# Attention tiles laid out by when they are first written, in a fused attention and recurrence block on one Trainium2 core

## The chip, the cores and the metric

The kernel runs on one core of one Trainium2 chip, as a single launch. Times are device microseconds (us) of that core. The kernel before was timed in three runs: 908.11, 908.41 and 908.92 us, median 908.41 us. One further run was profiled; it took 910.35 us, and the profile's span of it is 908.6 us.

## The reference

One layer of a decoder block over 1024 tokens of width 1024, batch 1, all in f32:

```python
h = rmsnorm(x, norm_g) * (1 + scale) + shift            # shift, scale, gate = c @ w_ada + b_ada
q, k, v, g_attn, xr, g_rnn, m_attn, m_rnn = split(h @ w_in)
y_attn = window_attention(rope(q), rope(k), v, sinks) * silu(g_attn)   # 16 heads of 64, 4 kv heads,
                                                                       # window 128, blocks of 128
y_rnn  = rg_lru(conv4(xr)) * silu(g_rnn)
merged = sigmoid(m_attn) * (y_attn @ w_attn_proj) + sigmoid(m_rnn) * (y_rnn @ w_rnn_proj)
out    = rmsnorm(x + gate * (merged @ w_out), final_g)
```

## The kernel before

**Products.** TensorE (PE) computes f32 products as three products of float32r parts. ScalarE (ACT) rounds an operand to its high part (`cast`, L106), VectorE (DVE) or GpSimd (POOL) subtracts to get the low part (`rest`, L112), and PE multiplies high by high, low by high and high by low. The input projection is done in pairs of column chunks, each pair in seven half-size products (a Strassen-like scheme, L711). Branch results go out to DRAM through a ring of five staging tiles named `c` (pool `stp`).

**Order of the work.** The order on every engine is written out by hand (`manual_schedule`). Four stages follow one another: the norms and the input projection; the recurrence, which runs in the shadow of the projection (`after_gates`, L1034, with tiles `it`, `rz`, `av`, `th`); the attention, mixed with the last projection products and then with the recurrence's output projection (`rp_steps`, L1468; product line L175); and the attention's output projection, the merge and the last product.

**The attention** is a loop over 32 units `u` (L1693): 4 groups of heads times 8 blocks of 128 queries. The parts of a unit lie in different turns of the loop, so that PE always has something: turn `u` has

- `scores(u)` on PE (L1337, psum tile `s_ps`), the copy of the scores by ACT into a tile `p` (L1344), the mask and row maxima by DVE (L1349, L1352), and for unit `u-1` the exponentials (ACT, L1357) and their normalization (DVE, L1363 and L1364);
- one piece of filler work on PE: twelve projection products (L711), and later twelve products of `rp_steps` (L175), which read `yh`, `yl`, the recurrence's output, loaded back from DRAM;
- `transposed(u-2)` on PE (L1371, `pt`), the split of the result into `phc` by ACT (L1376) and `plc` by DVE (L1382), and `pm`, masked copies of both, by POOL (L1393);
- `values(u-3)` on PE (L1407, `pv`), joined through `ob` (ACT, L1414) into a tile `yq` (DVE, L1425 and L1426).

Once a pair of units is joined, `a_prep` (L1530) multiplies `yq` by the gate path (DVE, L1537), rounds it into `ah` (ACT, L1542) and subtracts for `al` (DVE, L1547). These gated outputs are kept for the last stage: seven tiles of 8 KB a partition each, `ah` and `al` for groups 0 to 3 (the last low part lies elsewhere), all from the pool `hpool`, under one tag `H` with seven buffers (L1475).

**Transfers.** SyncE's queue (SP) carries the loads of queries and keys (`qs`, `ks`, one pair of tiles for two units, issued three turns ahead), of weights (`r`), gates and `yh`, `yl`; its DMAs take eight semaphores in turn, and each waits for the one eight before it to land. POOL's queue carries the loads of the values (`vb`, and `vd`, differences of neighbouring blocks), one of each per unit, the stores of the recurrence's last `yh`, `yl` (from `av` and `it`), and four late stores `smr_d` from the ring `c` (L1724): these have no place on SP's queue, and leave when POOL comes to them.

**Memory.** Pools are opened and closed as stacks, so the attention's tiles lie where tiles of earlier stages lay. A first write into such a place waits for the last use of each tile that lay there, a store's landing included (`reuse_waits="tile"`, L72). `open_attn` (L1286) opens the attention's pools in this order from the top of memory: `kq1`, `yo` (`pm`, `ob`, `yq`), `pp` (`p`, `small`, `neg`), `at` (`vb`, `vd`, `phc`, `plc`). In the built program `p` then overlaps `it`, which the last `yl` store reads, and the first `al` overlaps three buffers of the ring `c`, two of which late `smr_d` stores read.

**The end.** `load_b` (L1775) splits the seven blocks of the last weight. Six of them take buffers of `hpool` (two each), in the order in which `ah` and `al` come free.

Of the kernel before, what the change touches and what calls it, by code (L numbers as in the profile page):

```python
# [12 lines left out]
F32 = mybir.dt.float32  # L13
F32R = mybir.dt.float32r
# [8 lines left out]
P = 128  # L23
S = 1024
D = 1024
KC = 8
HALF = 512
# [28 lines left out]
def tile_hybrid_block(ctx, tc, x, pk, rows, posr, posi, c_row, w_ss, w_gate, w_main, w_v,  # L56
# [4 lines left out]
    def dma(dst, src, eng=nc.sync):  # L61
        dst, src = (a.bitcast(F32) if a.dtype == F32R else a for a in (dst, src))
        return eng.dma_start(dst, src)  # L63

    def f32(ap):
        return ap.bitcast(F32)
# [4 lines left out]
    def pool(st, name, bufs=1, **kw):  # L71
        return st.enter_context(tc.tile_pool(name=name, bufs=bufs, reuse_waits="tile", **kw))  # L72
# [76 lines left out]
    hh, hl, full = [], [], {}  # L149
# [16 lines left out]
    def mm_k(ps, w, kc, terms="hl", xh=hh, xl=hl):  # L166
        h, l = w[kc // 4]
        c0 = (kc % 4) * P
        w_h, w_l = h[:, c0:c0 + P], l[:, c0:c0 + P]
        prods = [(w_h, xh), (w_l, xh)] if "h" in terms else []  # L170
        if "l" in terms:
            prods.append((w_h, xl))
        for ww, xx in prods:
            for hf in range(2):
                mm = T.matmul(ps[hf], ww, xx[kc][hf],  # L175
                              start=(kc == 0 and ww is w_h and xx is xh),
                              stop=(kc == KC - 1 and xx is xl))
        return mm
# [14 lines left out]
    with ExitStack() as st:  # L193
# [11 lines left out]
        for i in range(8):  # L205
            t = sp.tile([P, D], F32, tag="xt", name="xt", bufs=XT)
# [373 lines left out]
    W = {}  # L580
# [215 lines left out]
    def store(dst, src):  # L796

        if "att" in W:
            behind.append(lambda: dma(dst, src))
        else:  # L800
            dma(dst, src)

    def flush():
        while behind:
            behind.pop(0)()
# [476 lines left out]
    at_ctx, psx_ctx = ExitStack(), ExitStack()  # L1282
    at = psx = None
    U = {}

    def open_attn():  # L1286
        nonlocal at, psx
        psm_ctx.close()
        psx = pool(psx_ctx, "psx", space=PSUM)
        W["kq", 1] = pool(at_ctx, "kq1", side="right")  # L1290
        W["yo"] = pool(at_ctx, "yo", side="right")
        W["pp"] = pool(at_ctx, "pp", bufs=3, side="right")
        W["pp"].tile([P, 64], F32, name="pad", bufs=1)
        W["neg"] = W["pp"].tile([P, 8], F32, name="neg", bufs=1)
        G.memset(W["neg"][:], -1e30)
        at = pool(at_ctx, "at", side="right")
        load_kq(1)
        for u in range(4):
            load_v(u)
            load_d(u)  # L1300

    def load_kq(m):
        g, t0 = m // 4, (m % 4) * 256
        ks = W["kq", m % 2].tile([P, 3, 2, P], F32R, tag="ks", name="ks")
        kv = k_d.rearrange("(p j) n b t -> j p n b t", j=4)[g]
        n0 = t0 // P
        lo = 1 if t0 == 0 else 0
        dma(ks[:, lo:, :, :], kv[:, n0 - 1 + lo:n0 + 2, :, :])
        qs = W["kq", m % 2].tile([P, 4, 256], F32R, tag="qs", name="qs")
        dma(qs[:], q_d[g][m % 4].rearrange("(a j) t -> a j t", j=4))  # L1310
        U["kq", m] = ks, qs

    def load_v(u):
        vb = U["v", u] = at.tile([P, P], F32R, tag="vb", name="vb", bufs=5)
        dma(vb[:], vs_d[u // 8][:, u % 8, :], G)

    def load_d(u):
        if u % 8:
            vd = U["d", u] = at.tile([P, 2, P], F32R, tag="vd", name="vd", bufs=4)
            dma(vd[:], dv_d[u // 8][:, u % 8, :, :].unsqueeze(0).to_broadcast([2, 64, 2, P]), G)  # L1320
# [51 lines left out]
        U["t", u] = [pt[:].rearrange("p l j q -> p (l j q)")]  # L1372

    def split_a(u):
        phc = at.tile([P, HALF], F32R, tag="phc", name="phc")
        A.copy(phc[:], U["t", u][0])  # L1376
        U["t", u].append(phc)

    def split_d(u):
        pt, phc = U.pop(("t", u))  # L1380
        plc = at.tile([P, HALF], F32R, tag="plc", name="plc")
        V.tensor_tensor(out=plc[:], in0=pt, in1=f32(phc[:]), op=ALU.subtract)  # L1382
        U["m", u] = phc, plc

    def masks(u):
        phc, plc = U["m", u]
        if u % 8:
            pm = W["yo"].tile([P, HALF], F32R, tag="pm", name="pm")
            lo, hi = slice(0, 256), slice(256, HALF)
            for to, s_, from_, cols in ((TOP, phc, TOP, lo), (END, phc, END, hi),  # L1390
                                        (END, plc, TOP, lo), (TOP, plc, END, hi)):
                d = 1 if cols is lo else -1
                G.affine_select(out=pm[to, cols], in_=f32(s_[from_, cols]),  # L1393
                                pattern=[[0, 4], [d, 64]], compare_op=ALU.is_ge, fill=0.0,
                                base=min(d, 0), channel_multiplier=-d)
            U["m", u] = phc, plc, pm
# [13 lines left out]

    def join_a(u):
        pvv = U["pv", u][0]
        ob = W["yo"].tile([P, 2, 2, 64], F32, tag="ob", name="ob")
        A.copy(ob[0:64], pvv[64:128, :, :, 0, :])  # L1414
        A.copy(ob[64:128], pvv[0:64, :, :, 1, :])
        U["pv", u].append(ob)
# [51 lines left out]
    def rp_steps():  # L1468
        h_ctx.close()
        pb_ctx.close()  # L1470
        psr = pool(ps_ctx, "psr", space=PSUM, side="right")
        rp_acc.extend(psr.tile([P, S], F32, name=f"rp{i}") for i in range(2))
        W["yp"] = pool(ctx, "ypool", bufs=12)
        W["tout"] = pool(ctx, "tout", bufs=1)
        W["hpool"] = pool(ctx, "hpool", bufs=7)  # L1475

        def part(c, kc2):
            for kc in (2 * kc2, 2 * kc2 + 1):
                W["pe"] = mm_k([rp_acc[c % 2][:, t] for t in SL], (O.get((c, 0)), O.get((c, 1))),
                               kc, xh=yh, xl=yl)  # L1480

        def finish(c):
            def f():
                flush()
                t = W["tout"].tile([P, S], F32, tag="rp", name="rp32")
                A.copy(t[:], rp_acc[c % 2][:])
                store(tr_d[c], t[:])
            later_a.append(f)
            if "att" not in W:
                do_later()  # L1490

        seq = [(c, k) for k in range(4) for c in range(2)]
        seq += [(c, k) for c in range(2, KC) for k in range(4)]
        load_y(2)
        load_y(3)
        for i, (c, k) in enumerate(seq):
            part(c, k)
            if i in (1, 2, 3, 4):
                load_y(i + 3)
            if i in (1, 2):  # L1500
                prep_r(i - 1, 1)
            if i in (6, 10):
                finish(0 if i == 6 else 1)
            if i >= 8 and k == 1 and c > 2:
                finish(c - 1)
            if i % 4 == 2:
                load_r((i + 2) // 4 + 1)
            if i >= 4 and i % 4 < 2:
                prep_r((i + 4) // 4, i % 4)
            yield  # L1510
        finish(7)
# [1 line left out]
    AH, AL = [], []  # L1513

    def a_alloc():
        for nm, g in (("ah", 0), ("al", 1), ("ah", 1), ("al", 0), ("ah", 2), ("al", 2), ("ah", 3)):
            U[nm, g] = W["hpool"].tile([P, 2, S], F32R, tag="H", name=nm)
        for lst, nm in ((AH, "ah"), (AL, "al")):
            lst.extend([[U[nm, g][:, a, t_] for t_ in SL] for a in range(2)]
                       for g in range(NG) if (nm, g) in U)  # L1520
        t = [W["hpool"].tile([P, HALF], F32R, name="al6", bufs=1)]
        t += [wp.tile([P, HALF], F32R, tag="ws", name="al7", bufs=3) for i in range(3)]
        AL.append([[t[2 * a + i][:] for i in range(2)] for a in range(2)])
# [239 lines left out]
    hpool, ypool = W["hpool"], W["yp"]  # L1763
# [8 lines left out]
    tpool = pool(ctx, "tpool", bufs=2)  # L1772
    ahh, alh = [[lst[c // 2][c % 2] for c in range(KC)] for lst in (AH, AL)]

    def load_b(j, pool, tag):  # L1775
        res = []
        for i in range(2):
            r = tpool.tile([P, 2, HALF], F32, tag="wr", name="wo32", bufs=2)
            dma(r[:], wo_d[j][2 * i:2 * i + 2].rearrange("k p n -> p k n"))
            t = pool.tile([P, 2, 2, HALF], F32R, tag=tag, name="wo")  # L1780
            A.copy(t[:, 0], r[:])
            V.tensor_tensor(out=t[:, 1], in0=r[:], in1=f32(t[:, 0]), op=ALU.subtract)
            res += [(t[:, 0, a, :], t[:, 1, a, :]) for a in range(2)]
        return res
# [14 lines left out]
    for c in range(KC):  # L1799
# [11 lines left out]
        if c < 4:  # L1811
            t = ypool.tile([P, S], F32, tag="Y", name="m_lo")
        else:
            t = tpool.tile([P, S], F32, tag="M", name="m_hi", bufs=4)
# [248 lines left out]
```

## Time and profile before

| | |
|---|---|
| median of three runs | 908.41 us |
| the profiled run | 910.35 us |
| its span in the profile | 908.6 us |
| PE busy | 894.8 us (98%) |
| DVE busy | 717.5 us (79%) |
| ACT busy | 567.7 us (62%) |
| POOL busy | 184.9 us (20%) |
| moved by DMA | 182.94 MB |

PE is busy in nearly all of the span, so the time can change only where PE stands still or runs at a lower clock. The attention begins at about 560 us and ends at about 737 us. In the profile's rows, an arrow `<-` behind a time names what ended the wait ahead of an instruction, `PEclk` is the clock granted to TensorE as a share of full speed, and the DMA share is the mean busy share of the 16 DMA engines (a little over 1 where their packets overlap).

### The profile page before, as it was taken

How to read it: one execution, taken by the hardware profiler on the slowest of the kernel's cores; microseconds unless marked ns; L12 is line 12 of the kernel's file. 1: busy time of each engine (PE TensorE's matmuls, PEld its weight loads, DVE VectorE, ACT ScalarE, POOL GpSimd, SP SyncE). 2: the span in 40 equal slices, each digit the busy share in tenths (PEclk: the TensorE clock that was granted, in tenths of full speed). 3: DMA queues.
4: the chain of work that ended last, by engine and by line, in shares of the span. 5: the costliest groups of instructions: out<-in, count | busy, mean ns of one | idle time of the engine just before them, and what ended most of it. 6: DMA issues, size and time to landing. Idle time of an engine off the chain costs nothing. (4 is left out here: it accounts for less than half of the span.)

```text
span 908.6 us, 12863 instructions
## 1 busy us (share of the span) xinstructions
PE 894.8 (98%) x4315; PEld 749.0 (82%) x4315; DVE 717.5 (79%) x1063; ACT 567.7 (62%) x1098; POOL 184.9 (20%) x331
## 2 busy tenths in 40 slices
PE   8999999999999999999999999989999999999997
PEld 6789888888888888888888888878888888888886
DVE  5987697989859875987789597979999836678855
ACT  6966455555557856686486884878888833115535
POOL 6420151100000000000000002478787720000000
PEclk9999999999999999999999999999999999999999
DMA  9819579773443353354446357999777379416504
GB/s 361 326 57 280 184 234 307 249 242 139 168 145 139 127 199 123 131 176 164 162 145 220 107 190 240 348 354 279 201 223 227 123 292 356 142 66 232 209 1 185
DMA packets 94837, 182.94 MB, mean 201 GB/s; under 512 B 15618, under 2 KB 36114, under 8 KB 94772
## 3 DMA queue, kind: packets, MB, share of 16 engines
q1 hardware_dynamic: 83200, 167.07, 53.1%
q0 software_dynamic: 11424, 14.80, 5.9%
q8 instruction: 34, 0.56, 0.2%
q14 instruction: 31, 0.25, 0.1%
q10 hardware_dynamic: 148, 0.27, 0.1%
HBM read 123.17 MB, written 59.21 MB: 201 GB/s over the span
## 5 line engine op out<-in xcount | busy, mean ns | idle before, releaser
L711 PE MATMUL bk<-nh,wh 128*128 128x512 f32 x368 | 143.3, 389 | 0.0
L711 PE MATMUL bk<-nl,wh 128*128 128x512 f32 x368 | 143.2, 389 | 0.0
L711 PE MATMUL bk<-nh,wl 128*128 128x512 f32 x368 | 98.4, 389 | 0.0
L106 ACT CAST wh<-r 128x512 fp32r<-128x512 f32 x107 | 65.5, 618 | 28.0 <-PE rp L175 12.9
L711 PEld LDWEIGHTS bk<-nh,wl 128*128 128x128 f32 x368 | 69.1, 188 | 14.4
L711 PEld LDWEIGHTS bk<-nl,wh 128*128 128x128 f32 x368 | 69.1, 188 | 14.2
L711 PEld LDWEIGHTS bk<-nh,wh 128*128 128x128 f32 x368 | 69.1, 188 | 14.2
L112 DVE TENSOR_TENSOR wl<-r,wh 128x512 fp32r<-128x512 f32 x91 | 62.1, 690 | 23.4 <-ACT wh L106 23.3
L63 POOL DMA_DIRECT2D yh_d<-av x1 | 0.6, 571 | 357.5 <-ACT av L1094 357.5
L711 PE MATMUL bk<-hl,wh 128*128 128x512 f32 x184 | 71.6, 389 | 0.0
L711 PE MATMUL bk<-hh,wh 128*128 128x512 f32 x184 | 71.6, 389 | 0.0
L112 DVE TENSOR_TENSOR wl<-ws,wh 128x512 fp32r<-128x512 f32 x76 | 52.0, 684 | 11.6 <-ACT wh L106 11.5
L106 ACT CAST wh<-ws 128x512 fp32r<-128x512 f32 x76 | 45.9, 615 | 7.7 <-PE bk L711 3.5
L1357 ACT ACTIVATE p<-p,small 128x129 f32<-128x129 f32 x128 | 50.0, 396 | 0.0
L711 PE MATMUL bk<-hh,wl 128*128 128x512 f32 x184 | 49.2, 389 | 0.0
L711 PEld LDWEIGHTS bk<-hh,wl 128*128 128x128 f32 x184 | 34.5, 188 | 7.2
L711 PEld LDWEIGHTS bk<-hl,wh 128*128 128x128 f32 x184 | 34.6, 188 | 7.1
L711 PEld LDWEIGHTS bk<-hh,wh 128*128 128x128 f32 x184 | 34.6, 188 | 7.1
L1337 PE MATMUL s_ps<-ks,qs 128*128 128x256 f32 (+1 forms) x256 | 36.8, 287 | 0.8 <-ACT p L1344 0.6
L1337 PEld LDWEIGHTS s_ps<-ks,qs 128*128 128x128 f32 x256 | 33.5, 195 | 3.2 <-DVE p L1349 1.9
L711 PE MATMUL bk<-hha,wh 128*128 128x512 f32 x92 | 35.8, 389 | 0.0
L711 PE MATMUL bk<-hla,wh 128*128 128x512 f32 x92 | 35.8, 389 | 0.0
(379 smaller groups left out, 2387.2 us busy)
## 6 DMA issues: line engine op xcount, KB each, us to landing
r<-w_main SPq DMA_DIRECT2D x100, 256.0 KB, 4.3
wada<-w_ss SPq DMA_DIRECT2D x16, 512.0 KB, 8.9
qs<-q_d SPq DMA_DIRECT2D x16, 512.0 KB, 7.2
wo_d<-wr SPq DMA_DIRECT2D x28, 256.0 KB, 2.5
wo<-wo_d SPq DMA_DIRECT2D x14, 512.0 KB, 5.9
ks<-k_d SPq DMA_DIRECT2D x12, 384.0 KB, 6.2
xt<-x SPq DMA_DIRECT2D x8, 512.0 KB, 7.9
sma_d<-c SPq DMA_DIRECT2D x16, 256.0 KB, 4.5
```

The source lines that it names most:

```text
L63: return eng.dma_start(dst, src)
L106: A.copy(dst[0][:], src)
L112: eng.tensor_tensor(out=dst[1][:], in0=src, in1=f32(dst[0][:]), op=ALU.subtract)
L711: W["pe"] = T.matmul(ps, ww[:, kc * P:(kc + 1) * P], b[kc][i], start=(first and n == 0), stop=(n == 11), skip_group_check=not first)
L1337: W["pe"] = T.matmul(o, qs[:, j, qc], ks[:, kb:n % 2 + 2, b, :], start=(b == 0), stop=(b == 1))
L1357: A.activation(px[:, j, :], px[:, j, :], AF.Exp, bias=sm[:, 0, j:j + 1], accum_out=sm[:, 1, j:j + 1])
```

## The change

Nothing is computed otherwise, and no instruction is moved, added or dropped: PE has 4301 instructions before and after, and they and those of DVE, ACT, POOL and SP stand in the same order. What changes is where tiles lie, and so what a first write into a tile waits for.

- The attention's pools are opened in the order `kq1`, `pp`, `vb` (tiles `vb`, `ob`), `hl` (`phc`, `plc`, `pm`), `yo` (`yq`), `at` (`vd`). `p` now lies over tiles of earlier chunks of the recurrence, `plc` and `pm` lie over `it`, and `yq` over `av`.
- `hpool` has six buffers under `H`, and one under a new tag `L`. The first `al` takes `L`, which lies over operands of the projection; the ring `c` now lies below `al` and `ah` of group 1.
- `load_b` gives the second and the ninth weight tile that it takes from `hpool` the buffer `L`, the others `H`.

```diff
@@ open_attn
         W["kq", 1] = pool(at_ctx, "kq1", side="right")
-        W["yo"] = pool(at_ctx, "yo", side="right")
         W["pp"] = pool(at_ctx, "pp", bufs=3, side="right")
         W["pp"].tile([P, 64], F32, name="pad", bufs=1)
         W["neg"] = W["pp"].tile([P, 8], F32, name="neg", bufs=1)
         G.memset(W["neg"][:], -1e30)
+        for nm in ("vb", "hl", "yo"):
+            W[nm] = pool(at_ctx, nm, side="right")
         at = pool(at_ctx, "at", side="right")
...
-        vb = U["v", u] = at.tile([P, P], F32R, tag="vb", name="vb", bufs=5)
+        vb = U["v", u] = W["vb"].tile([P, P], F32R, tag="vb", name="vb", bufs=5)
...
-        phc = at.tile([P, HALF], F32R, tag="phc", name="phc")
+        phc = W["hl"].tile([P, HALF], F32R, tag="phc", name="phc")
...
-        plc = at.tile([P, HALF], F32R, tag="plc", name="plc")
+        plc = W["hl"].tile([P, HALF], F32R, tag="plc", name="plc")
...
-            pm = W["yo"].tile([P, HALF], F32R, tag="pm", name="pm")
+            pm = W["hl"].tile([P, HALF], F32R, tag="pm", name="pm")
...
-        ob = W["yo"].tile([P, 2, 2, 64], F32, tag="ob", name="ob")
+        ob = W["vb"].tile([P, 2, 2, 64], F32, tag="ob", name="ob")
@@ rp_steps
-        W["hpool"] = pool(ctx, "hpool", bufs=7)
+        W["hpool"] = pool(ctx, "hpool", bufs=6)
@@ a_alloc
-        for nm, g in (("ah", 0), ("al", 1), ("ah", 1), ("al", 0), ("ah", 2), ("al", 2), ("ah", 3)):
+        U["al", 0] = W["hpool"].tile([P, 2, S], F32R, tag="L", name="al", bufs=1)
+        for nm, g in (("ah", 0), ("ah", 1), ("al", 1), ("ah", 2), ("al", 2), ("ah", 3)):
             U[nm, g] = W["hpool"].tile([P, 2, S], F32R, tag="H", name=nm)
@@ load_b
+            if pool is hpool:
+                in_l.append(len(in_l) in (1, 8))
+                tag = "L" if in_l[-1] else "H"
...
-            t = pool.tile([P, 2, 2, HALF], F32R, tag=tag, name="wo")
+            t = pool.tile([P, 2, 2, HALF], F32R, tag=tag, name="wo",
+                          bufs=1 if tag == "L" else None)
```

On DVE, at the first write of `al`, this stood before (an instruction, its result and operands, and in brackets the semaphores it waits for: `DMASW` are those of POOL's DMAs, `DMAHW` those of SP's):

```order
L1425 TENSOR_TENSOR yq_5911<-pv_5897,ob_5908 64x2x2x64 [waits PE_49,Activation_49]
L1426 TENSOR_TENSOR yq_5911<-pv_5897,ob_5908 64x2x2x64
L1547 TENSOR_TENSOR al_5861<-yq_5574,ah_5858 128x2x256 [waits DMASW5_49,DMASW4_49,DMASW1_49]
L1537 TENSOR_TENSOR yq_5721<-yq_5721,r_5659 128x512 [waits DMAHW3_49]
L1349 COPY_PREDICATED p_5914<-mgt_772,neg_5300 128x4x128 [waits Activation_49]
```

And this stands there now:

```order
L1426 TENSOR_TENSOR yq_5917<-pv_5903,ob_5914 64x2x2x64 [waits PE_49,Activation_49]
L1427 TENSOR_TENSOR yq_5917<-pv_5903,ob_5914 64x2x2x64
L1549 TENSOR_TENSOR al_5864<-yq_5580,ah_5865 128x2x256
L1539 TENSOR_TENSOR yq_5727<-yq_5727,r_5665 128x512 [waits DMAHW3_49]
L1350 COPY_PREDICATED p_5920<-mgt_772,neg_5297 128x4x128 [waits Activation_49]
```

The instructions are the same ones; the first `al` has lost its three waits on POOL's DMAs, which `ah` and `al` of group 1 have taken over, four pairs of units later.

On POOL, where the attention opens, this stood before (loads of `vb` and `vd`, then `p`'s last column):

```order
L1295 MEMSET neg 128x8 [waits DMAHW5_49,DMAHW3_49,DMAHW6_49,DMAHW2_49,DMAHW7_49,DMAHW0_49,PE_49]
L63 DMA vb<-vs_d_85 128x128 [waits DMAHW6_49,DMASW5_49]
L63 DMA vb<-vs_d_85 128x128 [waits DMASW6_49]
L63 DMA vd<-dv_d_89 128x1x256 [waits DMASW7_49]
L63 DMA vb<-vs_d_85 128x128 [waits DMASW0_49]
L63 DMA vd<-dv_d_89 128x1x256 [waits DMASW3_49,DMASW1_49,PE_49]
L63 DMA vb<-vs_d_85 128x128 [waits DMASW2_49]
L63 DMA vd<-dv_d_89 128x1x256
L1325 COPY p<-pk_t 128x4 [waits DMAHW3_49,DMAHW4_49,DMAHW0_49,DMAHW7_49,DMASW4_49,PE_49]
```

And now:

```order
L1294 MEMSET neg 128x8
L63 DMA vb<-vs_d_85 128x128 [waits DMASW5_49]
L63 DMA vb<-vs_d_85 128x128 [waits DMASW6_49]
L63 DMA vd<-dv_d_89 128x1x256 [waits DMAHW6_49,DMASW7_49,PE_49]
L63 DMA vb<-vs_d_85 128x128 [waits DMASW0_49]
L63 DMA vd<-dv_d_89 128x1x256 [waits DMASW1_49]
L63 DMA vb<-vs_d_85 128x128 [waits DMASW2_49]
L63 DMA vd<-dv_d_89 128x1x256 [waits DMASW3_49]
L1326 COPY p<-pk_t 128x4 [waits DMAHW5_49,DMAHW7_49,DMAHW4_49,DMAHW3_49]
```

The order is again the same. `p` no longer waits for `DMASW4`, the landing of the last `yl` store; the first `plc` on DVE waits for it now, and the first `yq` waits for the landing of the last `yh` store.

More of the change, by code (lines that the diff above doesn't have):

```diff
@@ L1773, in tile_hybrid_block @@
     ahh, alh = [[lst[c // 2][c % 2] for c in range(KC)] for lst in (AH, AL)]
+    in_l = []
     def load_b(j, pool, tag):
```

## The prediction

> **What bounds the kernel now.** I read the page first: its busy times and its picture in 40 slices.
>
> ```profile
> span 908.6 us, 12863 instructions
> PE 894.8 (98%) x4315; PEld 749.0 (82%) x4315; DVE 717.5 (79%) x1063; ACT 567.7 (62%) x1098; POOL 184.9 (20%) x331
> PE   8999999999999999999999999989999999999997
> ```
>
> TensorE (PE) works in 98% of the span. Away from both ends its row drops below 9 only in the 27th slice, 590.6 to 613.3 us (a slice is 908.6 / 40 = 22.7 us), within the attention. So I asked for PE's waits in the attention, 540 to 740 us:
>
> ```profile
> PE pt L1371 <- DVE plc L1382: 2.7, 1, 2.7
> PE s_ps L1337 <- ACT p L1344: 0.6, 1, 0.6
> PE pv L1407 <- ACT p L1357: 0.2, 1, 0.2
> PE pv L1407 <- POOL pm L1393: 0.2, 1, 0.2
> ```
>
> All that a new layout can win is in these four rows, and in what the longer one does to PE's clock. The timeline around the two shows who is late behind whom:
>
> ```profile
> 556.67 0.55 POOL L63 DMA_DIRECT2D yl_d<-it  x1 [1.89 <-DVE it L1098]
> ...
> 564.30 0.59 ACT L1344 COPY p<-s_ps 128x512 f32<-128x512 f32 x1 [5.05 <-DMA yl_d<-it]
> ...
> 564.93 1.21 PE L1337 MATMUL s_ps<-ks,qs 128*128 128x256 f32 x8 [0.61 <-ACT p L1344]
> ```
>
> The store of the last `yl` is issued at 556.67; ACT may not write `p`, which lies over its source, until it lands, and stands 5.05 us. PE has projection products to do meanwhile and loses 0.61 us.
>
> ```profile
> 594.29 1.10 POOL L63 DMA_DIRECT2D smr_d<-c  x2
> ...
> 604.97 0.69 DVE L1547 TENSOR_TENSOR al<-yq,ah 128x512 fp32r<-128x512 f32 x1 [4.83 <-DMA smr_d<-c]
> ...
> 607.48 1.32 POOL L1393 TENSOR_SCALAR_AFFINE_SELECT pm<-phc 64x256 fp32r<-64x256 f32 x2 [4.49 <-ACT phc L1376]
> ...
> 608.55 0.69 DVE L1382 TENSOR_TENSOR plc<-pt,phc 128x512 fp32r<-128x512 f32 x1
> ...
> 609.30 0.66 PE L1371 MATMUL pt<-ident,p 128*128 128x128 f32 x4 [2.74 <-DVE plc L1382]
> ```
>
> The late `smr_d` stores, the last two issued from 594.29, hold DVE's first `al` for 4.83 us. Behind it in DVE's order stand the masks and `plc`, and PE's transposes wait for `plc`: PE is idle from 606.56 (609.30 less 2.74) to 609.30. POOL stands 4.49 us in the same jam.
>
> The idle stretch costs twice. The next view cuts the time into stretches of 3.41 us, along the steps in the granted clock (columns: length, PE busy, weight loads, DVE, ACT, POOL, then clock, DMA share and GB/s):
>
> ```profile
> 22.78:26.19 3.41, 2.59 (x17) 1.57 (x16) 3.38 (x6) 2.85 (x7) 3.10 (x5) 1.00 1.03 395
> 26.19:29.60 3.41, 3.41 (x8) 2.76 (x9) 3.29 (x6) 3.38 (x6) 3.08 (x4) 0.50 1.03 409
> 562.08:565.49 3.41, 2.80 (x14) 2.06 (x13) 0.52 (x1) 1.19 (x3) 0.52 (x4) 1.00 1.04 334
> 565.49:568.90 3.41, 3.40 (x18) 2.56 (x16) 3.31 (x6) 3.12 (x12) 0.00 (x0) 1.00 1.05 247
> 606.46:609.87 3.41, 0.67 (x5) 0.42 (x4) 3.23 (x7) 3.35 (x9) 1.75 (x4) 1.00 1.03 367
> 609.87:613.28 3.41, 3.21 (x15) 3.07 (x15) 3.21 (x6) 2.31 (x9) 3.34 (x5) 0.50 1.04 403
> ```
>
> A stretch with PE busy for 0.67 us is followed by one at half clock, and so is one with 2.59 us; after 2.80 us the clock stays full. A half-clock stretch full of work loses 3.41 x 0.5 = 1.71 us.
>
> **What goes.** The edits to pools and tags cost no instruction on any engine: the order is the same, only waits differ. (a) `p` no longer waits for the `yl` store. ACT stood free for those 5.05 us, so it can write `p` long before 564.30, and PE's 0.61 us go. `plc` takes this wait over, but writes first ten microseconds after the store's landing at 564.2 (556.67 + 7.5, below); the same holds for `yq` and the `yh` store: 0. (b) The first `al` waits for nothing. DVE's run from `al` to the end of `plc` takes 609.24 - 604.97 = 4.27 us; from 604.97 - 4.83 = 600.14 it ends at 604.41, before PE is there (605.95), so DVE holds PE no longer. The waits for the `smr_d` stores pass to group 1's tiles, four pairs of units on, when the stores have long landed: 0. (c) `load_b`: its buffers come free in the same order, at the same products: 0.
>
> **What is late next.** The chain of waits gives the pace of a turn at full clock, and the slowed one:
>
> ```profile
> 611.78 1.76 PE s_ps L1337 x8
> ...
> 616.29 0.44 PE pt L1371 x4
> 616.73 0.71 PE pv L1407 x6
> 617.44 0.96 PE s_ps L1337 x8
> ...
> 622.08 1.22 PE s_ps L1337 x8
> ```
>
> With (a), PE ends its products at 606.56 - 0.61 = 605.95, does transposes and values in 0.44 + 0.71 us and reaches the scores of unit 10 at 607.10. These need the queries of that pair. Their load, and two that matter a little later, in SP's queue:
>
> ```profile
> 593.94 0.44 SPq L63 DMA_DIRECT2D qs<-q_d  x1
> ...
> 610.25 0.32 SPq L63 DMA_DIRECT2D qs<-q_d  x1
> ...
> 612.28 0.32 SPq L63 DMA_DIRECT2D yl<-yl_d  x1
> ```
>
> And their times to landing (the last column), asked for one by one, with the `yl` store's:
>
> ```profile
> qs<-q_d SPq DMA_DIRECT2D x1, 512.0 KB, 15.0
> ...
> qs<-q_d SPq DMA_DIRECT2D x1, 512.0 KB, 9.7
> ...
> yl<-yl_d SPq DMA_DIRECT2D x1, 512.0 KB, 11.3
> ...
> yl_d<-it POOLq DMA_DIRECT2D x1, 512.0 KB, 7.5
> ```
>
> The queries land at 593.94 + 15.0 = 608.94. So PE, freed from DVE, waits 608.94 - 607.10 = 1.84 us for a transfer instead. Would the transfer come earlier too? SP's own waits and the DMA's load say little:
>
> ```profile
> SPq L63 <- DMA yl<-yl_d: 4.0, 3, 1.8
> SPq L63 <- DMA yh<-yh_d: 3.7, 3, 1.4
> ...
> 570.00:575.00 5.00, 5.00 (x31) 4.33 (x30) 4.83 (x10) 4.25 (x14) 0.19 (x1) 1.00 0.95 320
> 575.00:580.00 5.00, 5.00 (x30) 4.29 (x29) 4.40 (x9) 4.71 (x16) 2.00 (x5) 1.00 1.04 391
> ...
> 620.00:625.00 5.00, 4.97 (x29) 3.95 (x28) 4.81 (x8) 4.45 (x17) 2.86 (x6) 1.00 1.05 254
> ...
> 555.00:630.00 75.00, 71.13 (x398) 60.63 (x398) 61.83 (x108) 54.75 (x169) 47.29 (x86) 0.98 1.02 329
> ```
>
> From 585 to 630 SP waits for the landings of its own earlier loads (first two rows), and the 16 DMA engines are full from 555 to 630 (share 1.02). The one gap is 570 to 575, at 0.95: 0.07 x 5 = 0.35 us that earlier requests could fill. I take 0.3.
>
> The sum by then, against the profiled run: scores of unit 10 end at 613.54 before (611.78 + 1.76) and at 608.94 + 0.96 = 609.90 after, 3.64 us earlier. But a stretch with some 1.84 us of idling has PE busy for about 1.57 of 3.41 us, less than the 2.59 that halved the clock: I count a half-clock stretch for it, 1.71 us, and 3.64 - 1.71 = 1.93 us are left.
>
> Two turns later the loads bind again. The queries of unit 12 land at 610.25 + 9.7 = 619.95 and are used at 622.08: 2.13 us of slack. The last `yl` lands at 612.28 + 11.3 = 623.58 and is first read here:
>
> ```profile
> 625.43 0.39 PE L175 MATMUL rp<-yl,wh 128*128 128x512 f32 x1
> ```
>
> That is 1.85 us of slack, the smallest; PE can't be ahead by more than this plus what the load gains. The load also loses: POOL, no longer standing for 4.49 us, issues the next unit's `vd` and `vb` (128 and 64 KB) about a turn earlier, ahead of `yl`. At 329 GB/s they take 0.6 us of all engines; but where such loads are under way the rate falls from 391 to 254 GB/s, and the 1.27 MB of those five microseconds would take 3.25 us at 391: 1.75 us lost to about two pairs, 0.9 each, 1.2 at most with rounding against me. I take 0.9. So the stream comes 0.9 - 0.3 = 0.6 us later, and PE's lead is 1.85 - 0.6 = 1.25 us, from 625 us on. Behind it the DMA empties, PE is full to the last product, and the lead stays: 909.1 instead of 910.35 for the profiled run. Nothing in it hangs on the profiler, so I take the same off the median: 908.4 - 1.2 = **907.2 us**. Its own range is 905.6 to 908.6: the stream 1 us earlier than I think (+0.3, less than a pair lost), up to 1.4 us later.
>
> A rule speaks otherwise of the clock. The Trainium skill, TensorE: Matmul & The Clock Gate, section "HAM oscillation — how this bites in real kernels", states that only gaps of PE over about 3.4 us matter. Against it stand the rows: 2.74 us of idling in one stretch were followed by half clock. By the rule neither the wait of 1.84 us nor a later one would slow PE; the lead at unit 10 would be 3.64 us, the loads of unit 12 would still cut it to 1.25, and the rival with a second slow stretch would be gone.
>
> **Rivals.**
>
> *A second half-clock stretch (18%).* If the stream comes two pairs later rather than one, 2 x 1.2 - 0.3 = 2.1 us, the lead at unit 12 is 1.85 - 2.1 = -0.25 us, and PE idles there for 1.93 + 0.25 = 2.2 us, within a stretch; the next one costs 1.71 us that no later load hides. Lost: 1.96 us, 910.4 us, slower. It decides once PE idles more than 0.6 to 0.8 us in one stretch near 620 us (2.80 busy is safe, 2.59 not). For it: POOL, which stood 4.49 us, will issue earlier throughout. Against it: where the first wait was followed by half clock, PE comes late to unit 12 and finds little to wait for.
>
> *The transfers move with the engines (22%).* If loads land earlier by what the engines gain, DVE's jam is all that was wrong: PE wins 0.61, 2.74, the 0.2 us behind it, and the half clock, in all 0.61 + (613.54 - 606.56 - 0.44 - 0.71 - 0.96) = 5.5 us: 902.9 us. A half-way case, with one wait of under 0.6 us and no slow stretch, gives about 904.7. For it: `qs` waits for PE's scores before it is issued. Against it: a share of 1.02 and 15 us to landing.
>
> *The change does nothing that counts (10%).* The stores are waited for by another first write (`plc`, `yq`), or PE loses again in unit 10 all that it won: 908.4 us.
>
> **The numbers.** A measurement of this kernel can tell about 0.2% from no change, 1.8 us: faster is below 906.6, slower above 910.2. The forecast has 50%; 1 us of its own range's 3 is below 906.6, at the thinner edge, for which I take 0.14; the rest is same (0.36). Faster: 0.14 + 0.22 = 0.36. Same: 0.36 + 0.10 = 0.46. Slower: 0.18. The range leaves out the better half of the second rival and most of the worse half of the first: 904.6 to 910.3.
>
> **What would show it.** Right, if `al` and ACT's first `p` wait for no DMA, DVE is busy from 600 to 605, and PE's longest waits in the attention are for `qs` (near 607 us, 1 to 2 us) and for `qs` or `yl` near 620, with one stretch at half clock after the first. Wrong in step (b), if DVE or POOL still hold `pt`; wrong on the loads, if `qs<-q_d` of unit 10 lands by 607 or PE stands nowhere above 0.6 us; wrong on the clock, if a wait of 1.5 us leaves it full.

## The result, and the profile after

| | runs | median, us | lowest to highest |
|---|---|---|---|
| before | 21 | 908.07 | 905.88 to 909.10 |
| after | 21 | 909.62 | 907.51 to 911.08 |

The ratio after to before is 1.0019, with a 95% interval of 1.0012 to 1.0026. The change makes the kernel 1.6 us slower; the forecast was 907.2 us, 1.2 us faster. The time lies inside the range of 904.6 to 910.3 us, but on the wrong side of no change.

The profiled run of the changed kernel took 907.51 us, the fastest of its 21. Its page shows a span 2.8 us shorter than before, and PE's one slice below 9 away from the end a place later (611 to 634 us; a slice is 905.8 / 40 us):

```profile
span 905.8 us, 12857 instructions
PE 891.5 (98%) x4314; PEld 746.1 (82%) x4315; DVE 718.2 (79%) x1063; ACT 568.1 (63%) x1098; POOL 185.1 (20%) x331
PE   9999999999999999999999999998999999999997
```

Two profiles don't start alike, so I compare them from the first product of unit 0's scores to that of unit 13's, past the crowded part. Their timeline rows, of the kernel before:

```profile
560.49 0.33 PE L1337 MATMUL s_ps<-ks,qs 128*128 128x128 f32 x2
...
627.03 0.28 PE L1337 MATMUL s_ps<-ks,qs 128*128 128x256 f32 x1
```

and of the changed one:

```profile
558.19 0.33 PE L1338 MATMUL s_ps<-ks,qs 128*128 128x128 f32 x2
...
624.18 0.40 PE L1338 MATMUL s_ps<-ks,qs 128*128 128x256 f32 x2
```

That is 66.54 us before and 65.99 us after. From there to the end of the span it is 281.6 us in both (908.6 - 627.03, 905.8 - 624.18). So of the 2.8 us 2.3 lie ahead of the attention, where no instruction was changed, and this run gained 0.55 us. PE's waits in the attention, 540 to 740 us, after:

```profile
PE s_ps L1338 <- DVE yq L1427: 3.0, 1, 3.0
PE s_ps L1338 <- DMA qs<-q_d: 1.4, 1, 1.4
PE s_ps L1338 <- DVE p L1365: 0.5, 1, 0.5
```

Both longer waits of the kernel before are gone. In their place PE waits for the queries of unit 10 (1.4 us) and of unit 12 (3.0 us). The row of 3.0 us names DVE, because `yq` (L1427) happens to end just then, at 618.65. But the scores don't read `yq`, and DVE had read the last scores out of `s_ps` by 615.67 (L1350). The load of that pair, PE's rows in the timeline, and the load's time to landing show what it was:

```profile
607.18 0.32 SPq L63 DMA_DIRECT2D qs<-q_d  x1
...
606.02 1.19 PE L1338 MATMUL s_ps<-ks,qs 128*128 128x256 f32 x8 [1.37 <-DMA qs<-q_d]
618.76 1.19 PE L1338 MATMUL s_ps<-ks,qs 128*128 128x256 f32 x8 [3.04 <-DVE yq L1427]
...
qs<-q_d SPq DMA_DIRECT2D x1, 512.0 KB, 11.4
```

The queries land at 607.18 + 11.4 = 618.6 us, and PE starts at 618.76; the other profiles below have the same 0.13 to 0.15 us between this landing and PE's start, wherever PE waits for it. Nor do the first two `al` wait for a transfer, nor the first copy of scores (timeline, DVE and ACT):

```profile
597.13 0.88 DVE L1549 TENSOR_TENSOR al<-yq,ah 128x512 fp32r<-128x512 f32 x1
602.66 0.87 DVE L1549 TENSOR_TENSOR al<-yq,ah 128x512 fp32r<-128x512 f32 x1
...
559.23 0.59 ACT L1345 COPY p<-s_ps 128x512 f32<-128x512 f32 x1 [2.83 <-PE s_ps L1338]
```

This run gained, most don't. What they lose is looked for in the clock, below.

### The profile page after: what moved, and what is told of

Same layout as the page of the kernel before. It is cut to its first block, busy times and chain, and to the rows that moved or that the text cites. A ratio compares the mean times of both kernels' runs of the same rounds, so it can differ in the third digit from the quotient of the medians.

```text
span 905.8 us, 12857 instructions
## 1 busy us (share of the span) xinstructions
PE 891.5 (98%) x4314; PEld 746.1 (82%) x4315; DVE 718.2 (79%) x1063; ACT 568.1 (63%) x1098; POOL 185.1 (20%) x331
## 4 chain that ended last, share of the span: by engine, by line
PE 91%; DVE 3%; DMA 3%; ACT 1%; POOL 1%; issue 1%; DVEq 0%; ACTq 0%; SPq 0%
PE bk L711 48%; PE rp L175 13%; PE out L1874 6%; PE pmain L175 5%; PE pgate L1027 5%; PE s_ps L1338 3%; PE bk L487 3%; PE pmain L487 2%; PE pv L1408 2%; DMA r<-w_rp 1%; DMA yl<-yl_d 1%; PE pt L1372 1%; PE pmain L1581 1%; PE pmain L1580 1%; PE pmain L1579 1%; PE bk L258 1%
## 5 line engine op out<-in xcount | busy, mean ns | idle before, releaser
L711 PEld LDWEIGHTS bk<-nh,wh 128*128 128x128 f32 x368 | 69.1, 188 | 14.2
L711 PEld LDWEIGHTS bk<-nl,wh 128*128 128x128 f32 x368 | 69.1, 188 | 14.2
```

The costliest lines, as they stand in the source:

```text
L711: W["pe"] = T.matmul(ps, ww[:, kc * P:(kc + 1) * P], b[kc][i], start=(first and n == 0), stop=(n == 11), skip_group_check=not first)
```

## The experiments

Theory A: with DVE free, PE comes to the queries before they land; it stands there for 3 to 4 us in one piece, and that wait halves its clock in most runs. Rivals: B, the loads are later and the clock has no part in it; C, the new order of pools costs the time; D, the reordered loads of the later experiments are worth their gain without the change; E, latency, not bytes, sets when a load lands. Ratios are to the kernel before, timed on the same chip.

**The changed kernel again** (no edit).

> The changed kernel once more, as it is. Theory A (TensorE now waits for the queries of units 10 and 12 instead of VectorE, and either wait may halve its clock for a stretch or two): median near 909.6 us, with runs at a mean clock of 0.996 to 0.997 at 907.5 to 908.7 us and runs at 0.992 to 0.994 at 909 to 911 us; the profile shows waits for qs of about 1.4 and 3 us, and a slow profiled run has half-clock stretches right behind them. Theory B (the loads land a microsecond later, and the clock has no part in it): the same median, but the time does not follow the clock.

Measured: 910.08 us, ratio 1.0025 (1.0015 to 1.0035). The profiled run took 908.93 us, the third fastest of 9. PE's rows at units 10 and 12, then at units 0 and 13, and the stretches of 3.41 us along the steps in the clock:

```profile
604.45 1.19 PE L1338 MATMUL s_ps<-ks,qs 128*128 128x256 f32 x8 [0.62 <-DVE small L1364]
618.19 2.04 PE L1338 MATMUL s_ps<-ks,qs 128*128 128x256 f32 x8 [4.04 <-DMA qs<-q_d]
...
557.66 0.22 PE L1338 MATMUL s_ps<-ks,qs 128*128 128x128 f32 x1
...
625.57 0.28 PE L1338 MATMUL s_ps<-ks,qs 128*128 128x256 f32 x1
...
613.30:616.71 3.41, 0.86 (x6) 0.42 (x4) 3.23 (x8) 2.10 (x6) 1.82 (x4) 1.00 1.09 302
616.71:620.12 3.41, 1.93 (x9) 1.96 (x10) 1.08 (x2) 0.00 (x0) 3.13 (x5) 0.50 1.06 268
620.12:623.54 3.42, 3.42 (x10) 2.65 (x10) 2.30 (x4) 2.65 (x10) 0.00 (x0) 0.50 1.06 312
```

The wait of 4.04 us is followed by two stretches at half clock: the same eight products take 2.04 us instead of 1.19. Half of the busy time there, (1.93 + 3.42) / 2 = 2.7 us, is lost, and this run needs 625.57 - 557.66 = 67.9 us from unit 0 to unit 13, 1.4 us more than before. (The 0.62 us at unit 10 are a wait for queries too: they land at 590.21 + 14.1 = 604.3 us.) In the first profile of the changed kernel the wait at unit 12 was a microsecond shorter and fell otherwise into the stretches:

```profile
603.73:607.15 3.42, 2.05 (x17) 1.87 (x16) 3.27 (x7) 1.32 (x3) 3.23 (x6) 1.00 1.02 369
613.97:617.39 3.42, 1.75 (x10) 1.14 (x8) 3.25 (x6) 2.86 (x10) 1.73 (x4) 1.00 1.05 296
617.39:620.80 3.41, 2.04 (x13) 1.90 (x14) 2.14 (x5) 0.94 (x4) 2.88 (x6) 1.00 1.08 282
```

Its 3.04 us are cut in two by a boundary, PE is busy for 1.75 and 2.04 us of the two stretches, and the clock stays full. The 30 timed runs of the changed kernel in both sets say how often the clock is low: 23 have a mean clock of 0.994 or less and a median of 910.1 us, 7 have 0.996 or more and a median of 908.4 us. Of the 110 runs of the kernel before that were timed beside the experiments, 6 have 0.994 or less. The mean clock doesn't say where the slow stretches lie: those at the start, and the tail behind the last product (in the first profile PE ends at 899.3 us, and the clock is at half from 904.1), count in it too. That they lie behind the wait in the runs that took 910 us is inferred from the profiles here, none of which is of such a run.

**PE kept busy while it waits**, first at units 10 and 12, then at unit 12 alone (8 products in place of the table):

```diff
@@ scores
+        for _ in range({10: 4, 12: 9}.get(u, 0)):
+            T.matmul(s_full[:, 0:HALF], yh[0][0][:, 0:P], yh[0][1], start=True, stop=True)
```

> The changed kernel with 4 extra products ahead of the scores of unit 10 and 9 ahead of those of unit 12 (128x512, written into the psum tile that these scores then overwrite; nothing of the result depends on them): TensorE is busy while the queries come. Theory A: no half-clock stretch in the attention, mean clock 0.996 to 0.997 in nearly every run, and a median of 907.5 to 908.3 us although TensorE does 5 us more. Theory B: the median stays at 909.6 us or goes above it, since the extra products can only add.

> The changed kernel with 8 extra products (128x512, 3.1 us) ahead of the scores of unit 12 alone, written into the psum tile that these scores overwrite. Theory A: the 3 to 4 us of standing still become 3.1 us of work and at most 1 us of waiting, so no half-clock stretch follows: mean clock 0.996 to 0.998 in nearly every run, median 907.3 to 908 us, 2 us below the change alone although TensorE does more. Theory B (the clock has no part in it): 909.6 to 911 us.

Measured: 908.83 us, 1.0016 (1.0003 to 1.0028), and 908.09 us, 1.0008 (0.9999 to 1.0017). With 3 to 5 us of work added, the median is 1.2 to 2 us below that of the changed kernel in the run before, where work alone could only add. The first interval overlaps that of the changed kernel, the second barely (0.9999 to 1.0017 beside 1.0015 to 1.0035); the clocks differ more clearly, as 21 of these 23 runs have 0.996 or more, against 7 of 30. With the half-clock stretches behind the wait, above, B falls. But the first is above what was expected, and the second a little. In both profiles the queries came later, and a wait was left that had been expected to be 1 us at most. In the first, 2.00 us of it sufficed for a half-clock stretch:

```profile
616.10:619.51 3.41, 1.41 (x9) 0.93 (x8) 2.22 (x5) 0.41 (x1) 2.88 (x6) 1.00 1.09 276
619.51:622.93 3.42, 3.42 (x13) 2.94 (x12) 1.43 (x2) 2.15 (x10) 0.99 (x1) 0.50 1.03 318
```

In the second, a border of the stretches cut the 2.13 us that were left, and the clock stayed full:

```profile
615.33:618.74 3.41, 1.89 (x8) 1.20 (x7) 3.33 (x7) 1.50 (x4) 2.67 (x5) 1.00 1.09 285
618.74:622.15 3.41, 2.80 (x16) 2.53 (x17) 0.86 (x3) 1.57 (x7) 2.09 (x3) 1.00 1.05 296
```

In both, unit 12's scores start 61.7 us after unit 0's (619.07 - 557.36, 619.35 - 557.62), against 60.5 to 60.6 in the changed kernel's two (618.19 - 557.66, 618.76 - 558.19). Why the queries land a microsecond later there is open.

**The two halves of the change, one at a time.** First the order of the attention's pools alone, then the edits to `hpool`, `a_alloc` and `load_b` alone (each is the diff of the change without the other's lines).

> The kernel before with the change's order of the attention's pools alone; al stays over the ring of the late smr_d stores. Theory A (the loads are the limit once VectorE no longer is): PE's wait for p of 0.6 us goes, the hold at al stays, and the landing of its stores moves by less than 0.7 us: 907.2 to 908.0 us beside 908.1 for before. Theory C (some other effect of the new order of pools costs the time): 909 to 910 us.

> The kernel before with the edits to hpool, al and load_b alone; p still lies over the source of the yl store. Theory A: VectorE is free at al, POOL loads vd and vb 5 us earlier, the queries of unit 12 land about 1 us later than in before, and TensorE comes to them with a lead that is 0.6 us smaller than after the whole change: one wait of 2.5 to 3.5 us at unit 12, median 908.7 to 910 us. Theory C: 908 us or less, the loss being the pools'.

Measured: 907.21 us, 0.9994 (0.9986 to 1.0003), and 909.29 us, 1.0018 (1.0008 to 1.0027). The pools cost nothing, so C falls; all of the loss is on the half that frees `al`. With the pools alone DVE's hold stays, and with it PE's wait and its half-clock stretch (DVE's row, PE's wait, the stretches):

```profile
601.12 0.69 DVE L1548 TENSOR_TENSOR al<-yq,ah 128x512 fp32r<-128x512 f32 x1 [4.63 <-DMA smr_d<-c]
...
PE pt L1372 <- DVE plc L1383: 2.5, 1, 2.5
...
602.05:605.46 3.41, 0.91 (x5) 0.41 (x4) 3.24 (x7) 2.95 (x7) 1.25 (x2) 1.00 1.03 339
605.46:608.88 3.42, 3.42 (x15) 3.23 (x16) 3.21 (x7) 2.81 (x11) 3.28 (x5) 0.50 1.04 402
```

With `al` alone free, the waits are those of the whole change, and the border of the clock shows:

```profile
PE s_ps L1337 <- DMA qs<-q_d: 4.5, 2, 3.4
...
612.84:616.26 3.42, 1.87 (x11) 1.22 (x9) 3.25 (x6) 2.86 (x11) 1.74 (x4) 1.00 1.06 301
616.26:619.67 3.41, 1.52 (x11) 1.47 (x12) 2.07 (x5) 0.55 (x2) 2.89 (x6) 1.00 1.08 272
619.67:623.09 3.42, 3.42 (x10) 2.65 (x9) 2.31 (x4) 2.34 (x10) 0.85 (x1) 0.50 1.04 334
```

**POOL's loads one turn later**, on top of the change and in the kernel before:

```diff
-        if 3 <= u < 31:
-            load_d(u + 1)
-            load_v(u + 1)
+        if 4 <= u < 32:
+            load_d(u)
+            load_v(u)
```

> The changed kernel with vd and vb of each unit loaded one turn later (three turns ahead of use instead of four): one pair of them, some 0.9 us of the stream by the prediction's estimate, goes behind the queries of unit 12. Theory A: waits for qs 0.9 us shorter, median about 908.7 us. If POOL's loads do not weigh on SP's: 909.6 us. If three turns are too few for them: TensorE waits for vb or vd in every unit of the crowded part, over 911 us.

> The kernel before with vd and vb of each unit loaded one turn later. Theory A: the loads of queries come earlier by a little under 1 us, but VectorE's hold at al sets TensorE's time there, not the loads; vd itself may come late by up to 1 us in the crowded part as it did with the whole change. Same as before within 0.5 us (907.3 to 908.5), so that the later loads are worth 3 us behind the change and nothing ahead of it. Theory D (the later loads of vd are worth 1 to 3 us by themselves): 905 to 907 us.

Measured: 907.04 us, 0.9996 (0.9987 to 1.0005), and 907.99 us, 1.0006 (0.9997 to 1.0015). One pair of small loads moved behind the queries of unit 12 takes 2.6 to 3.0 us off the changed kernel's median and nothing off the one before: D falls for this edit. PE waits for `vd` now (rows of the changed kernel with the edit), but ahead of unit 12, where it has time. The wait of 1.67 us at unit 12, put down to DVE, ends with the queries' landing again (606.22 + 10.6 = 616.8):

```profile
PE pv L1408 <- DMA vd<-dv_d: 1.0, 2, 0.8
...
606.22 0.32 SPq L63 DMA_DIRECT2D qs<-q_d  x1
...
qs<-q_d SPq DMA_DIRECT2D x1, 512.0 KB, 10.6
...
557.49 0.22 PE L1338 MATMUL s_ps<-ks,qs 128*128 128x128 f32 x1
...
616.96 1.19 PE L1338 MATMUL s_ps<-ks,qs 128*128 128x256 f32 x8 [1.67 <-DVE p L1365]
```

The queries of unit 12 land 59.3 us after unit 0's first product (606.22 + 10.6 - 557.49), as against 60.4 in the changed kernel (618.6 - 558.19) and 59.5 before (619.95 - 560.49). In the kernel before, the edit moves that landing by as much, from 59.5 to 58.4 us, where nothing waits for it. So one pair of POOL's loads is worth about 1.1 us of landing time, and the change does bring one pair forward past the queries of unit 12, which SP issues at 610.25 before and at 607.18 after (POOL's rows before, then after):

```profile
610.15 0.83 POOL L63 DMA_DIRECT2D vd<-dv_d  x1
...
602.94 0.83 POOL L63 DMA_DIRECT2D vd<-dv_d  x1
```

That accounts for the 0.9 us by which the change's loads are late. With the edit the wait shrinks to 1.67 us, which left the clock full in this profile. The median gains more than the 0.9 us expected; 10 of the 11 runs have a mean clock of 0.996 or more, so the half-clock stretches go with the wait.

**The late stores later as well.** The edit was to hold the last two `smr_d` stores back to turn 12:

```diff
-        while own_stores:
+        while own_stores and (u < 7 or u >= 12):
```

> The changed kernel with vd and vb one turn later and the last two smr_d stores in turn 12 rather than 7: 0.52 MB, at 329 GB/s 1.6 us of all engines, behind the queries of unit 12 too. Theory A: of the waits for vd (1.4 us), qs (1.7 us) and yl (0.5 us) that were left with vd alone, 1.6 to 2.5 us go, nothing halves the clock: 904.5 to 906 us, faster than before (908.1) and than vd alone (907.0). Theory E (latency, not bytes): as vd alone, 907 us.

Measured: 907.12 us, 0.9995 (0.9986 to 1.0004). This decides nothing: the stores are handed to POOL in turn 6, and the edit moves no instruction. It is a repetition of the run above, and agrees with it. Holding back the stores of turn 6 themselves (`and (u < 6 or u >= 11)`, for which 907 to 908.3 us were expected) gave no time, as the queues of that program wait for one another without end; what those stores are worth is open.

**One pair of SP's loads later**, on top of the change, together with POOL's, and in the kernel before:

```diff
@@ rp_steps
-            if i % 4 == 2:
-                load_r((i + 2) // 4 + 1)
-            if i >= 4 and i % 4 < 2:
+            if i % 4 == 2 and i > 2 or i == 4:
+                load_r((i + 2) // 4 + 1)
+            if i in (6, 7):
+                prep_r(2, i - 6)
+            if i > 5 and i % 4 < 2:
                 prep_r((i + 4) // 4, i % 4)
```

> The changed kernel with one pair of SP's loads (the two halves of r from w_rp, 0.52 MB in all) issued behind the last yl instead of two positions ahead of the queries of unit 12, and its rounding two pieces later. Theory A: 0.52 MB at 329 GB/s are 1.6 us, so the queries of unit 12 and the last yl land about 1.6 us earlier; TensorE's wait at unit 12 falls from 3 to 4 us to 1.5 to 2.5 us, mostly without a half-clock stretch: 906 to 908 us beside 909.6 to 910.1 for the change alone. Theory E (transfers take their latency, bytes ahead of them do not count): 909.6 to 910.1 us.

> Both orders of loads in the changed kernel: r from w_rp behind the last yl, vd and vb one turn later. Theory A: the waits for qs (1.7 us) and yl (0.5 us) of the kernel with vd alone shrink by up to 1.6 us: 905.3 to 906.3 us, faster than before and than either alone. Theory E: as vd alone, 907.0 us.

> The kernel before with the two halves of r from w_rp issued behind the last yl, as in the run that gained 3 us on top of the change. Theory A (loads bind only where VectorE's hold at al is gone): VectorE still sets TensorE's time at unit 10, and the queries of unit 12 had 2 us of slack there, so nothing is won: 907.2 to 908.0 us beside 907.4 to 908.1 for before. Theory D (the order of loads is worth its 1 to 3 us by itself): 905 to 906.5 us.

Measured: 906.44 us, 0.9997 (0.9986 to 1.0009); 906.25 us, 0.9989 (0.9979 to 0.9998); 907.31 us, 0.9998 (0.9990 to 1.0007). In the kernel before the edit is worth nothing (D falls for this edit), in the changed one 3.2 to 3.6 us of the median; there the interval is wide, as one of the 12 runs took 910.34 us. The loads of unit 12 in the first of them:

```profile
601.45 0.32 SPq L63 DMA_DIRECT2D qs<-q_d  x1
...
qs<-q_d SPq DMA_DIRECT2D x1, 512.0 KB, 13.8
...
557.38 0.33 PE L1338 MATMUL s_ps<-ks,qs 128*128 128x128 f32 x2
...
615.37 0.36 PE L1338 MATMUL s_ps<-ks,qs 128*128 128x256 f32 x1 [2.15 <-DMA qs<-q_d]
...
612.37:615.78 3.41, 1.26 (x9) 0.85 (x8) 3.23 (x8) 1.32 (x3) 2.09 (x5) 1.00 1.08 286
615.78:619.20 3.42, 3.42 (x13) 2.93 (x12) 2.05 (x3) 2.10 (x10) 1.46 (x3) 0.50 1.09 248
```

The queries land 57.9 us after unit 0's first product, 2.5 us earlier than with the change alone; 1.6 were expected of 0.52 MB. This does not decide about E by itself, as two loads fewer stand ahead of the queries in SP's queue, and they are issued earlier too, 44.1 us after unit 0 (601.45 - 557.38) instead of 49.0 (607.18 - 558.19). The time to landing decides: it is not a fixed latency, but 13.8 us here and 11.4 with the change alone; and with POOL's edit the queries were issued at about the same time as without it (48.7 us after unit 0) and landed 1.1 us earlier, with one pair of loads fewer ahead. So what stands ahead of a load counts, and E falls. This profile still has a wait of 2.15 us in one stretch and a half-clock stretch behind it. With both orders no wait at unit 12 is left (PE's waits, second kernel; the 0.8 us are at unit 4, the first 0.6 us at unit 18):

```profile
PE pv L1408 <- DMA vd<-dv_d: 1.1, 1, 1.1
PE s_ps L1338 <- DVE p L1365: 0.8, 1, 0.8
PE s_ps L1338 <- DVE p L1350: 0.6, 1, 0.6
PE pv L1408 <- POOL p L1326: 0.6, 1, 0.6
```

It is the only version clear of the kernel before, by 0.02 to 0.21%. Not all of its lead lasts: unit 13 starts 63.7 us after unit 0, 2.3 us earlier than in the first profile of the change, but from there to the end this profile takes 283.0 us instead of 281.6, most of the difference at unit 18 (the profile names DVE; why it is late there was not looked into). Both orders together in the kernel before were not run, so D is ruled out for each edit alone, and not for the pair. In the kernel before with the later load, DVE's hold made PE wait 2.52 us, and the clock stayed full that time:

```profile
602.16:605.57 3.41, 1.49 (x7) 0.91 (x5) 3.24 (x7) 2.34 (x5) 1.16 (x2) 1.00 1.05 329
605.57:608.99 3.42, 2.16 (x14) 1.75 (x15) 3.24 (x6) 3.29 (x13) 2.77 (x6) 1.00 1.02 403
```

**Both orders, POOL's from unit 10 on only** (the condition above becomes `3 <= u < 32 and u != 9`, the unit `u + (u < 9)`).

> The changed kernel with r from w_rp behind the last yl and, from unit 10 on only, vd and vb loaded one turn later, so that the units before it have theirs in time. Theory A: the waits for vd of 1.7 us and for vb of 0.4 us that the later loads cost in units 5 to 7 go, the wait for the queries of unit 12 stays under 1.5 us: 904.8 to 906.0 us, clearly faster than before and a little faster than the two orders of loads together (906.25). Theory E: 906.4 us, as with r alone.

Measured: 906.72 us, 0.9993 (0.9984 to 1.0003). The waits for `vd` are gone as expected, and the time is not the 904.8 to 906.0 us expected with that: they had been ahead of unit 12, where PE waits for its queries in their stead.

```profile
PE s_ps L1338 <- DMA qs<-q_d: 2.2, 2, 1.5
```

## Why the prediction was wrong

- **Step (a), `p`; step (b), `al`; step (c), `load_b`: right.** No first `p` or `al` waits for a transfer, DVE holds PE at unit 10 no longer, and from unit 13 to the end the two profiles take the same 281.6 us.
- **The wait at unit 10: right in kind, too long.** 1.84 us were worked out; 1.37 and 0.62 us were measured. The queries came 47.7 and 46.7 us after unit 0 (591.64 + 14.2 - 558.19, 604.3 - 557.66), where the prediction kept the 48.5 of before (608.94 - 560.49). With the pools alone, DVE's hold still in place, they came at 47.3, so this needs no freed engine.
- **The half-clock stretch behind it: the step that failed.** "I count a half-clock stretch for it, 1.71 us" rested on a stretch of the start, where 2.59 us of busy PE were followed by half clock. In the attention, after stretches at full clock, 0.86, 0.91, 1.26, 1.41 and 1.52 us were followed by half clock, 1.49, 1.75, 1.87, 2.04 and more were not: the border lies near 1.5 us, less than half of a stretch. So neither wait at unit 10 cost anything more, and the sum took off 1.71 us that were not lost.
- **The lead at unit 12: too small by 2 to 3 us, 1.71 of them for that reason.** The sum left PE 1.93 us ahead; the rest of the error is mostly the shorter wait at unit 10. PE reached unit 12 57.5 us after unit 0 (618.76 - 3.04 - 558.19), and 56.5 in the second profile (618.19 - 4.04 - 557.66, the start of unit 0 there), where before it took 61.6: a lead of 4.1 to 5.1 us. The queries allow 1.2 us (61.6 - 60.4). The rest is one wait of 3 to 4 us. In the profiles it halved the clock for no stretch (3.04 us), for one (3.4 us, `al` alone) and for two (4.04 us), and nothing behind it hides them. So the half-clock stretch that the sum put at unit 10, where the later loads would have hidden it, came at unit 12.
- **The loads of unit 12: right in kind, a little small.** 0.6 us of lateness were worked out for the last `yl`; the queries of unit 12 came 0.9 us late (60.4 us after unit 0 in both profiles and 60.6 with `al` alone free, against 59.5 before and 59.2 with the pools alone), and bound first. That a pair of POOL's loads costs this was shown by moving it. So these transfers did not come earlier with the engines, as the second rival had it.
- **The rival that was taken as 18% is what happened.** A second half-clock stretch near 620 us was priced at 910.4 us; the runs with a low mean clock have 910.1. Its condition was wrong: the loads need not come two pairs late. It was enough that PE did not lose its lead at unit 10. That the price fits is luck in part: it was one stretch and 0.25 us of lost lead (1.71 + 0.25), where the slow profile has 1.2 us of lead and two stretches that lose 2.7.
- **Slips that decided nothing.** The stretch of 570 to 575 us was called the one gap of the DMA engines, but rows beside it have 0.99 at 585 to 590 and 0.92 at 625 to 630. And the lower end of the own range, 905.6 us, needs a lead of 2.8 us, where the sum had left 1.93.
- **The rule.** The Trainium skill, TensorE: Matmul & The Clock Gate, section "HAM oscillation — how this bites in real kernels", gives as its rule that PE should have no idle gaps over about 3.4 us, and by it the rival would be gone. The runs go against it: waits of 2.00, 2.15 and 2.5 us, each inside one stretch, halved the clock. That one of 3.04 us across a border did not is within the rule, but shows that the length of a gap does not decide by itself.

The start of each profile differs by up to 3 us, with half-clock stretches there in some and not in others; what sets them was not tried.

## What to carry to other kernels

When a stall goes, follow the freed engine to the next thing that it can't pull forward, and put the whole lead there: if that is a load on a full queue, the stall moves and may come back in one piece, longer than the two that were there. Take away bytes ahead of that load in the same change; here each order of later loads alone was worth nothing without the layout, the layout was a loss without them, and with both orders of loads it gained 0.11% (0.02 to 0.21%). Where a wait can halve the clock, add up PE's busy time in each stretch of the clock's grid, and read the border from stretches of the same kind of work.

## What the hardware showed

In these traces the clock changes only at the borders of stretches of 3.41 us, and the place of the borders differs from run to run: one of them lies 55.0 us after unit 0 in one profile (612.37 - 557.38) and 55.6 us in another (613.30 - 557.66). So waits of about the same length cost differently by where they fall: of those of 2.0 to 2.2 us one cost nothing (2.13 us) and two a half-clock stretch each (2.00 and 2.15), and of two of 2.5 us one cost nothing and one a stretch. With the stretches at the start, this is part of why one kernel's times spread over 3 to 4 us (907.5 to 911.1 us after, 905.9 to 909.1 before). One profile of such a kernel can be its luckiest run: the first one here was 2.1 us faster than its median. And products that compute nothing, put into the wait, brought the ratio to before from 1.0025 (1.0015 to 1.0035) to 1.0008 (0.9999 to 1.0017).
